# Three tiles per block, two roots together and sums on VectorE alone, in a hybrid decoder layer on one Trainium2 core

## The chip, the cores and the metric

The kernel runs on one core of one Trainium2 chip. The metric is device time in microseconds, the median of several executions. Beside it there is one profiled execution, whose trace gives the rows below. The engines are named as in the profile: PE is TensorE's matmul (PEld its weight load), DVE is VectorE, ACT is ScalarE, POOL is GpSimd, SP is SyncE, whose queue issues the DMAs.

## The reference

One inference step of a one-layer decoder over 1024 prompt tokens and 8 single new tokens, 1032 token columns in all, with a model width of 1024, in f32:

```python
u = rmsnorm(h, norm_mix)
proj = u @ w_in                       # RWKV-7 columns | gated DeltaNet columns | gates
o_a = ...                             # RWKV-7 time mixing from pa
o_b = ...                             # short conv and gated delta rule from pb
mix = gate_a * (o_a @ w_branch_a) + gate_b * (o_b @ w_branch_b)
h = h + mix @ w_out                   # residual
u2 = rmsnorm(h, norm_ffn)
h = h + (silu(u2 @ w_ffn_gate) * (u2 @ w_ffn_up)) @ w_ffn_down
h = h + sigmoid(rmsnorm(h, norm_ple) @ w_ple_gate) * (pe @ w_ple_proj)
y = rmsnorm(h, norm_final)
```

It also returns the new states of both mixers.

## The kernel before

**Layout.** Everything is held transposed: channels on the 128 partitions (KT = 8 channel tiles), tokens along the free dimension. The 1032 columns are cut into three blocks of BW = 344, or for the second half of the kernel into two halves of 516 and four quarters of QW = 258. Each f32 operand of a large product is split into a rounded high part and a rest (`split`, lines 245 to 250, for activations; `halves_of`, line 184, for weights, ScalarE for the high part, GpSimd for the rest), and three products hi·hi, lo·hi, hi·lo are summed. So one weight tile of `w_in` on one block is 24 matmuls of 344 columns. Split weights live in `wsp`, six buffers for each of `wh` and `wl`; a tile of `w_in` takes two of each.

**Order.** A planner orders the instructions of each engine ahead of time, by priority (`tc.cur_priority`, a lower number goes first) and by when it believes each is ready; adding LATER = 100000 puts work behind what is urgent. Each engine then runs its list strictly in order. In the head and in `order` (line 112) TensorE's list is the order in which the code is written.

**The head (lines 355 to 409).** `xs` holds the input. Per block, `gram(g)` puts the Gram matrices of its 128-token pieces on TensorE. `inv` takes the diagonal (product with `idr`, sum), the reciprocal square root by twelve small steps on 128x3 (`rsq`, lines 236 to 242), scales `idr` by it (`nre`, line 290), and a product with `ones` on TensorE spreads the result over all partitions; ScalarE copies it to `R`. `scale(g, R)` multiplies the eight channel tiles of the block by `R`, alternately on VectorE and GpSimd (line 391), and splits them into `xh` and `xl` (lines 249, 250). `stream` yields the products with `w_in` one matmul at a time; `dense_some(n)` lets n of them go. Its first two tiles are done block by block, all later ones tile by tile. The result is evacuated by ScalarE to `gs` and stored. Behind the head, `order` interleaves the rest of this stream with the two mixers.

**The residual and the FFN's input (lines 1436 to 1500).** `mixer_out(t)` does, for each half t, the product with `w_out` and the residual: VectorE adds x to the product (`H<-acc`, line 1468), the squares are summed over the channel tiles (`square`, line 1415), and a root as above gives `RN[t]`. `mixes(t)` scales H by `RN[t]` (line 1443, 8 operations of 516 columns) and forms the seven inputs of a Strassen product: 20 sums `ms` (line 1453) and 28 rests `xl` (line 1456) of 258 columns, alternately on VectorE and GpSimd, and 28 rounded copies on ScalarE. Between, the product with `w_ple_proj` (`dense(a["wpp"])`) runs; ScalarE evacuates it to `po`, two buffers of one block each, and SP stores it (lines 1497 to 1499). Then come the gate and up products (`strassen`): seven products per half, each of 12 matmuls of 258 columns; the first gate product takes the whole first half before the second.

**The FFN.** After a group of hidden tiles the product with `w_ffn_down` is added to the residual: each block is loaded into a tile `a`, added to (line 1611) and stored. `depth[0]` is the number of buffers of `a`.

Of the kernel before, what the change touches and what calls it, by code (L numbers as in the profile page):

```python
# [58 lines left out]
def hybrid(ctx, tc, a, o):  # L59
# [145 lines left out]
    def width(c):  # L205
        return c.stop - c.start
# [55 lines left out]
            G.tensor_copy(idr[:, t0:min(n, t0 + P)], ident[:, :min(P, n - t0)])  # L262
        return idr

    def inv_rms(R, ps, pl_, newps, grams=False):

        n = ps.shape[1]  # L270
        parts = [slice(t0, min(n, t0 + P)) for t0 in range(0, n, P)]
        e = pl_.tile([P, idr.shape[1]], F32, tag="nre", name="nre", bufs=2)
        r = pl_.tile([P, 3, 3], F32, tag="nrr", name="nrr", bufs=2)
        if grams:
            V.memset(r[:, 0], 1.0)
            for i, c in enumerate(parts):
                w = slice(0, width(c))
                tt(e[w, c], ps[w, c], idr[w, c], MULT)
                V.tensor_reduce(r[w, 0, i:i + 1], e[w, c], AX.X, ADD)
        else:  # L280
            tt(e[:, :n], ps, idr[:, :n], MULT)
            if n >= 2 * P:
                V.tensor_reduce(r[:, 0, 0:2], e[:, 0:2 * P].rearrange("p (i t) -> p i t", t=P), AX.X, ADD)
            for i, c in enumerate(parts):
                if n < 2 * P or i > 1:
                    V.tensor_reduce(r[:, 0, i:i + 1], e[:, c], AX.X, ADD)
        q = [r[:, i, :len(parts)] for i in range(3)]
        rsq(q[1], q[0], 1.0 / T, EPS, q[0], q[2])
        for i, c in enumerate(parts):
            ts(e[:, c], idr[:, c], r[:, 1, i:i + 1], None, MULT)  # L290
        pr = newps([P, n])
        mm(pr, ones, e[:, :n], start=True, stop=True)
        act(R, pr, AF.Copy)

    def stream(jobs):
# [38 lines left out]
            if b == NBLK - 1:  # L334
                mark(("pa", ti), 3.0)

        nxt = [fetch(ti) for ti in jobs[:2]]
        for b in range(NBLK):
            for ti, w in zip(jobs, nxt):
                yield from product(ti, *w, b)  # L340
        for n, ti in enumerate(jobs[2:], 2):
            if n == 2:
                nxt = fetch(ti)
            w = nxt
            tc.cur_priority -= LATER
            if n + 1 < len(jobs):
                nxt = fetch(jobs[n + 1])
            tc.cur_priority += LATER
            for b in range(NBLK):
                yield from product(ti, *w, b)  # L350
# [6 lines left out]
    with tc.tile_pool(name="ld", bufs=1, side="right", reuse_waits="tile") as ld, \  # L357
# [20 lines left out]
                    mm(ps[:w, t0:t0 + w], x, x, start=(k == 0), stop=(k == KT - 1))  # L378
            return ps

        def inv(g, ps):
            R = ld.tile([P, BW], F32, tag="R0", name="R0", bufs=2)
            tc.cur_priority -= 2 * LATER
            inv_rms(R, ps, ld, ft, True)
            tc.cur_priority += 2 * LATER
            return R

        def scale(g, R):
            c = cols(g)
            for k in range(KT):  # L390
                (gtt if k % 2 else tt)(xs[:, k, c], xs[:, k, c], R, MULT)
                split(xs[:, k, c], vc("nmix", k), xh[k][:, c], xl[k][:, c])

        def dense_some(n):
            for _ in range(n):
                next(dense_in)

        s0 = gram(0, ct([P, BW]))
        s1 = gram(1, ct([P, BW]))
        scale(0, inv(0, s0))  # L400
        dense_some(3 * KT)
        s2 = gram(2, st1([P, BW]))
        R = inv(1, s1)
        dense_some(3 * KT)
        scale(1, R)
        R = inv(2, s2)
        dense_some(6 * KT)
        scale(2, R)
        dense_some(6 * KT)
    w0h, a0h, kah, ka1 = vx[:, 0:4], vx[:, 4:8], vx[:, 8:12], vx[:, 12:16]  # L410
    ts(w0h, vc("w0", 0, 4), 0.5, None, MULT)
    ts(a0h, vc("a0", 0, 4), 0.5, None, MULT)
# [1023 lines left out]
    def mixes(pl_, t):  # L1436


        hi, lo = ([pl_.tile([P, 4, QW], F32R, tag=f"x{q}{i}", name=f"x{q}{t}{i}") for i in range(7)] for q in "hl")
        tc.cur_priority += LATER  # L1440
        y = []
        for m in range(KT):
            stt(H[t][m], H[t][m], vc("nffn", m), RN[t], MULT, MULT)  # L1443
# [1 line left out]
        for i in SIX:  # L1445
            for k in range(4):
                (y11, y12), (y21, y22) = y[k], y[k + 4]
                p, q, op = ((y11, y22, ADD), (y11, None, None), (y12, y22, SUB), (y21, y11, SUB),
                            (y22, None, None), (y11, y12, ADD), (y21, y22, ADD))[i]
                e, e2 = (gtt, tt) if k % 2 else (tt, gtt)  # L1450
                if op:
                    s = hq[t].tile([P, QW], F32, tag="ms", name="ms", bufs=3)
                    e(s, p, q, op)
                    p = s
                act(hi[i][:, k], p, AF.Copy)
                e2(lo[i][:, k], p, hi[i][:, k].bitcast(F32), SUB)
        tc.cur_priority -= LATER
        return hi, lo

    def mixer_out(t):  # L1460
# [30 lines left out]
    xb = pool(ctx, "xm1", 1)  # L1491
    XM[1] = mixes(xb, 1)
    sgp = pool(hstk, "sg", 1)
    sg = [sgp.tile([P, TOK], F32, name=f"sg{i}") for i in range(2)]
    for m in range(KT):
        def evac(b, ps, m=m):
            y = hq[1].tile([P, BW], F32, tag="po", name="po", bufs=2)
            act(y, ps, AF.Copy)
            SP.dma_start(pp_d[m, :, cols(b)], y)
        dense(a["wpp"][m], 2, ph, pl, evac)  # L1500

# [69 lines left out]
    for n in (2, 4, 4, 4, 4, 4):  # L1573
        for j in range(0, n, 2):
# [11 lines left out]
            if f0 + j == 0:  # L1586
# [1 line left out]
                hp = pool(hstk, "hid")  # L1588
                hh, hl = pair(hp, "hid", 4)
                tmp = pool(hstk, "tf", 2)  # L1590
                depth[0] = 5
            strassen(a["wu"], f0 + j, up)
        final = f0 + n == NF
        if final:
# [133 lines left out]
```

## Time and profile before

| | us |
|---|---|
| median of 3 runs | 2087.26 (2086.81 to 2088.21) |
| profiled execution, its own time | 2085.75 |
| span of its trace | 2084.0 |
| TensorE busy in the span | 1943.8 (93%) |
| VectorE, ScalarE, GpSimd busy | 1321.5, 845.0, 1045.1 |

The time of the profiled execution is 1.75 us more than the span of its trace: what lies around the first and the last instruction. "Busy" counts an operation from its start to its end, including time in which it stands still for a resource; matmuls overlap each other and their ends are modelled. The granted clock (PEclk) is a mean over a window, as a share of full speed; the clock has two levels, 1.2 and 2.4 GHz.

### The profile page before, as it was taken

To read this page: it belongs to the slowest core of one execution; us is meant where nothing else is said; L and a number is where in the kernel's file an instruction comes from. 1 tells how busy PE (TensorE), PEld (TensorE's weight loads), DVE (VectorE), ACT (ScalarE), POOL (GpSimd) and SP (SyncE) were. 2 spreads that over 40 slices of the span, in tenths; PEclk is the share of its full clock that TensorE was granted. 3 is DMA by queue.
4 is the path that set the end of the run, shared out by engine and by line. 5 is a ranking of instruction groups with operands and counts; after the bars stand their busy time and mean duration, and the time that the engine had idled before them with its cause. 6 is when DMAs were issued, how large, how long until landed. Compare 5 with 4: busy or idle time off the path is not lost.

```text
span 2084.0 us, 40641 instructions
## 1 busy us (share of the span) xinstructions
PE 1943.8 (93%) x14904; PEld 1819.6 (87%) x14904; DVE 1321.5 (63%) x3253; ACT 845.0 (41%) x2069; POOL 1045.1 (50%) x1144
## 2 busy tenths in 40 slices
PE   5988999899899997999799988999999999999996
PEld 5987878777777877989699978899999999999995
DVE  6269756987988549736644587464643636446767
ACT  2343353555555341237523355241433414234532
POOL 3366362556564244750047677463645536354722
PEclk8999899999999999999899998999999999999998
DMA  4433332243343433564445542625244262433312
GB/s 143 126 107 107 101 105 89 79 131 93 100 118 112 144 93 119 168 177 126 155 139 168 166 151 75 196 75 165 86 123 143 72 186 69 130 110 113 110 55 95
DMA packets 218497, 250.89 MB, mean 120 GB/s; under 512 B 48409, under 2 KB 176297, under 8 KB 218297
## 3 DMA queue, kind: packets, MB, share of 16 engines
q1 hardware_dynamic: 218296, 248.30, 39.4%
q8 instruction: 117, 1.92, 0.4%
q14 instruction: 84, 0.68, 0.1%
HBM read 170.82 MB, written 77.40 MB: 119 GB/s over the span
## 4 chain that ended last, share of the span: by engine, by line
PE 64%; DVE 21%; DMA 4%; ACT 4%; issue 4%; POOL 3%; SPq 0%; DVEq 0%; POOLq 0%; ACTq 0%
PE acc L75 54%; PE c L75 3%; PE f L75 3%; DVE GM L685 1%; PE zp L75 1%; DVE inv L721 1%; PE f L79 1%; PE s L75 1%; DVE L L574 1%; PE x L75 1%; DVE H L1443 1%; DMA a<-h_d 1%; DVE inv L722 1%; DVE LB L709 1%; DMA out_gdns<-St 1%
## 5 line engine op out<-in xcount | busy, mean ns | idle before, releaser
L75 PE MATMUL acc<-xh,wh 128*128 128x258 f32 (+2 forms) x2360 | 733.3, 311 | 13.1 <-ACT gs L328 5.7
L75 PE MATMUL acc<-xl,wh 128*128 128x258 f32 (+2 forms) x2360 | 728.0, 309 | 9.7 <-DVE xl L250 5.6
L75 PE MATMUL acc<-xh,wl 128*128 128x258 f32 (+1 forms) x2336 | 722.9, 310 | 0.0
L187 POOL TENSOR_TENSOR wl<-ws,wh 128x512 fp32r<-128x512 f32 (+1 forms) x256 | 334.7, 1309 | 440.2 <-ACT wh L186 408.3
L75 PEld LDWEIGHTS acc<-xh,wh 128*128 128x128 f32 (+1 forms) x2360 | 450.7, 191 | 22.8 <-ACT gs L328 6.0
L75 PEld LDWEIGHTS acc<-xl,wh 128*128 128x128 f32 (+1 forms) x2360 | 451.2, 191 | 18.3 <-DVE xl L250 6.4
L75 PEld LDWEIGHTS acc<-xh,wl 128*128 128x128 f32 x2336 | 448.5, 192 | 5.8 <-POOL wl L187 0.5
L186 ACT ACTIVATE wh<-ws 128x512 fp32r<-128x512 f32 (+1 forms) x256 | 157.2, 615 | 257.7 <-PE acc L75 217.3
L187 POOL TENSOR_TENSOR wl<-s,wh 128x512 fp32r<-128x512 f32 x110 | 145.0, 1320 | 124.4 <-ACT wh L186 123.6
L75 PE MATMUL acc<-hidh,wh 128*128 128x344 f32 x528 | 167.1, 320 | 4.6 <-DVE a L1611 4.0
L75 PE MATMUL acc<-hidl,wh 128*128 128x344 f32 x528 | 169.5, 321 | 0.0
L75 PE MATMUL acc<-hidh,wl 128*128 128x344 f32 x528 | 168.8, 320 | 0.0
L1611 DVE TENSOR_TENSOR a<-a,acc 128x344 f32<-128x344 f32 x120 | 60.9, 512 | 137.7 <-PE acc L75 92.8
L186 ACT ACTIVATE wh<-s 128x512 fp32r<-128x512 f32 x110 | 69.2, 630 | 141.0 <-PE acc L75 98.0
L1561 POOL TENSOR_TENSOR s<-ws 128x512 f32<-128x512 f32 x66 | 87.7, 1329 | 48.1 <-DMA ws<-in_wg 34.9
L75 PEld LDWEIGHTS acc<-hidh,wh 128*128 128x128 f32 x528 | 98.8, 188 | 6.8 <-DVE a L1611 5.2
L75 PEld LDWEIGHTS acc<-hidl,wh 128*128 128x128 f32 x528 | 99.3, 188 | 0.3 <-DVE hidl L247 0.3
L75 PEld LDWEIGHTS acc<-hidh,wl 128*128 128x128 f32 x528 | 99.3, 188 | 0.0
L445 POOL TENSOR_TENSOR cy<-cy,cu 128x344 f32<-128x344 f32 x72 | 68.8, 955 | 50.2 <-ACT cu L444 44.1
L75 PE MATMUL acc<-mxh,wh 128*128 128x258 f32 x256 | 72.7, 284 | 0.0
L75 PE MATMUL acc<-mxl,wh 128*128 128x258 f32 x256 | 72.6, 284 | 0.0
L75 PE MATMUL acc<-mxh,wl 128*128 128x258 f32 x256 | 72.2, 282 | 0.0
(464 smaller groups left out, 4074.2 us busy)
## 6 DMA issues: line engine op xcount, KB each, us to landing
ws<-in_win SPq DMA_DIRECT2D x92, 256.0 KB, 3.1
a<-h_d SPq DMA_DIRECT2D x120, 172.0 KB, 2.6
h_d<-a SPq DMA_DIRECT2D x120, 172.0 KB, 2.8
pa_d<-gs SPq DMA_DIRECT2D x90, 172.0 KB, 2.2
ws<-in_wg SPq DMA_DIRECT2D x44, 256.0 KB, 2.9
ws<-in_wu SPq DMA_DIRECT2D x44, 256.0 KB, 3.0
ws<-in_wd SPq DMA_DIRECT2D x40, 256.0 KB, 2.7
gate_d<-gs SPq DMA_DIRECT2D x48, 172.0 KB, 2.7
```

The lines of the kernel that those rows point to most:

```text
L75: last[0] = TE.matmul(out, w, x, start=start, stop=stop).ins
L79: last[0] = TE.transpose(out, x, ident).ins
L186: act(h, s, AF.Copy)
L187: (eng or gtt)(l, s, h.bitcast(F32), SUB)
L445: gtt(y, y, u, ADD)
L574: V.tensor_tensor_scan(L[:, c * C:c * C + C], ones[:, 0:C], L[:, c * C:c * C + C], 0.0, MULT, ADD)
L685: stt(GM[:, 2 * (c + j) + h], ps[h][:, j], cvf[:, cg, h:h + 1], rwmask, MULT, MULT)
L709: V.transpose(LB[0:32, i0:i0 + 16], G2[:, :, i0:i0 + 16].rearrange("p b i -> p i b"))
L721: tt(u[:, :i], XB[:, :i, :i], LB[:, 16 + i:17 + i, 16:16 + i].to_broadcast([P, i, i]), MULT)
L722: tt(w, XA[:, :ns, :nj], LB[:, i:i + 1, :nj].to_broadcast([P, ns, nj]), MULT)
L1561: e(s, A_[p], A_[q], op)
L1611: tt(y, y, ps, ADD)
```

## The change

- In the head, `inv` is replaced by `roots`, which takes a list of Gram blocks: the root of block 0 is taken alone, those of blocks 1 and 2 in one chain whose small steps work on 128x6. The three Gram products come first, and roots and first norming stand in a higher priority band. `scale` uses VectorE for all eight tiles.
- `stream` does three tiles block by block instead of two; `dense_some` is called with 6, 12 and 9 times KT matmuls between the steps, 216 in all instead of 144.
- `mixes` does all sums and rests on VectorE, and the first half's stand one more LATER behind (`(2 - t) * LATER`).
- `po` becomes two full-width tiles that later hold `sg`.
- The FFN's `a` has six buffers instead of five.

```diff
-        nxt = [fetch(ti) for ti in jobs[:2]]
+        nxt = [fetch(ti) for ti in jobs[:3]]
         for b in range(NBLK):
             for ti, w in zip(jobs, nxt):
                 yield from product(ti, *w, b)
-        for n, ti in enumerate(jobs[2:], 2):
-            if n == 2:
+        for n, ti in enumerate(jobs[3:], 3):
+            if n == 3:
                 nxt = fetch(ti)
...
-        def inv(g, ps):
-            R = ld.tile([P, BW], F32, tag="R0", name="R0", bufs=2)
-            tc.cur_priority -= 2 * LATER
-            inv_rms(R, ps, ld, ft, True)
-            tc.cur_priority += 2 * LATER
+        def roots(grams):
+
+            n = len(grams)
+            parts = [(g, i, min(P, BW - i * P), slice(i * P, min(BW, i * P + P))) for g in range(n) for i in range(3)]
+            e = ld.tile([P, n, BW], F32, name=f"e{n}")
+            r = ld.tile([P, 3, 3 * n], F32, name=f"r{n}")
+            V.memset(r[:, 0], 1.0)
+            for g, i, w, c in parts:
+                tt(e[:w, g, c], grams[g][:w, c], idr[:w, c], MULT)
+                V.tensor_reduce(r[:w, 0, 3 * g + i:3 * g + i + 1], e[:w, g, c], AX.X, ADD)
+            rsq(r[:, 1], r[:, 0], 1.0 / T, EPS, r[:, 0], r[:, 2])
+            R = []
+            for g, i, w, c in parts:
+                ts(e[:, g, c], idr[:, c], r[:, 1, 3 * g + i:3 * g + i + 1], None, MULT)
+                if i == 2:
+                    pr = ft([P, BW])
+                    mm(pr, ones, e[:, g], start=True, stop=True)
+                    R.append(ld.tile([P, BW], F32, name=f"R{n}{g}"))
+                    act(R[-1], pr, AF.Copy)
             return R

         def scale(g, R):
             c = cols(g)
             for k in range(KT):
-                (gtt if k % 2 else tt)(xs[:, k, c], xs[:, k, c], R, MULT)
+                tt(xs[:, k, c], xs[:, k, c], R, MULT)
                 split(xs[:, k, c], vc("nmix", k), xh[k][:, c], xl[k][:, c])
...
+        tc.cur_priority -= 2 * LATER
         s0 = gram(0, ct([P, BW]))
         s1 = gram(1, ct([P, BW]))
-        scale(0, inv(0, s0))
-        dense_some(3 * KT)
+        R0, = roots([s0])
         s2 = gram(2, st1([P, BW]))
-        R = inv(1, s1)
-        dense_some(3 * KT)
-        scale(1, R)
-        R = inv(2, s2)
+        scale(0, R0)
+        tc.cur_priority += 2 * LATER
         dense_some(6 * KT)
-        scale(2, R)
-        dense_some(6 * KT)
+        tc.cur_priority -= 2 * LATER
+        R1, R2 = roots([s1, s2])
+        scale(1, R1)
+        tc.cur_priority += 2 * LATER
+        dense_some(12 * KT)
+        scale(2, R2)
+        dense_some(9 * KT)
...
-        tc.cur_priority += LATER
+        tc.cur_priority += (2 - t) * LATER
         y = []
...
-                e, e2 = (gtt, tt) if k % 2 else (tt, gtt)
                 if op:
                     s = hq[t].tile([P, QW], F32, tag="ms", name="ms", bufs=3)
-                    e(s, p, q, op)
+                    tt(s, p, q, op)
                     p = s
                 act(hi[i][:, k], p, AF.Copy)
-                e2(lo[i][:, k], p, hi[i][:, k].bitcast(F32), SUB)
-        tc.cur_priority -= LATER
+                tt(lo[i][:, k], p, hi[i][:, k].bitcast(F32), SUB)
+        tc.cur_priority -= (2 - t) * LATER
...
-    sg = [sgp.tile([P, TOK], F32, name=f"sg{i}") for i in range(2)]
     for m in range(KT):
-        def evac(b, ps, m=m):
-            y = hq[1].tile([P, BW], F32, tag="po", name="po", bufs=2)
-            act(y, ps, AF.Copy)
-            SP.dma_start(pp_d[m, :, cols(b)], y)
+        po = sgp.tile([P, TOK], F32, tag=f"sg{m % 2}", name="po")
+
+        def evac(b, ps, m=m, po=po):
+            act(po[:, cols(b)], ps, AF.Copy)
+            SP.dma_start(pp_d[m, :, cols(b)], po[:, cols(b)])
         dense(a["wpp"][m], 2, ph, pl, evac)
+    sg = [sgp.tile([P, TOK], F32, tag=f"sg{i}", name=f"sg{i}") for i in range(2)]
...
-                depth[0] = 5
+                depth[0] = 6
```

## Rows read from the trace of the kernel before

**Rows 1.** Windows of the head: each engine's busy time, clock, DMA share, GB/s.
```profile
17.40:30.20 12.80, 2.87 (x7) 1.15 (x5) 12.65 (x24) 6.75 (x13) 11.14 (x10) 0.62 0.27 83
30.20:44.40 14.20, 14.17 (x94) 13.83 (x94) 7.82 (x21) 2.77 (x6) 4.16 (x4) 0.87 0.16 49
44.40:58.00 13.60, 5.92 (x19) 5.31 (x19) 11.21 (x28) 5.62 (x12) 5.38 (x6) 0.62 0.04 14
58.00:82.00 24.00, 24.00 (x155) 24.00 (x154) 9.33 (x25) 8.20 (x17) 9.93 (x11) 1.00 0.45 141
```

**Rows 2.** TensorE's waits from 0 to 125 us: total, times, longest.
```profile
PE f L75 <- DVE nre L290: 7.7, 1, 7.7
PE acc L75 <- DVE xl L250: 5.6, 2, 3.1
```

**Rows 3.** Head: first root's window on VectorE, then single timeline rows (start, length).
```profile
12.60:17.00 4.40, 3.82 (x21) 1.00 1.06 371
...
18.07 0.46 ACT L293 ACTIVATE R<-f 128x344 f32<-128x344 f32 x1 [0.70 <-PE f L75]
24.84 0.50 DVE L391 TENSOR_TENSOR xs<-xs,R 128x344 f32<-128x344 f32 x1
28.46 1.22 DVE L240 TENSOR_TENSOR nrr<-nrr 128x3 f32<-128x3 f32 x1
58.22 4.66 DVE L250 SCALAR_TENSOR_TENSOR xl<-xs,vec,xh 128x344 fp32r<-128x344 f32 x8
...
26.56 4.75 POOL L187 TENSOR_TENSOR wl<-ws,wh 128x512 fp32r<-128x512 f32 x3 [1.66 <-ACT wh L186]
...
35.19 4.98 PE L75 MATMUL s<-xs 128*128 128x128 f32 x48
```

**Rows 4.** ScalarE's timeline: two evacuations of the first stage, three products apart.
```profile
74.61 0.46 ACT L328 ACTIVATE gs<-acc 128x344 f32<-128x344 f32 x1 [3.01 <-issue]
...
85.95 0.46 ACT L328 ACTIVATE gs<-acc 128x344 f32<-128x344 f32 x1 [3.01 <-issue]
```

**Rows 5.** Windows from the second half's residual to the first down products.
```profile
1185.00:1213.70 28.70, 28.70 (x237) 28.47 (x236) 23.77 (x30) 13.38 (x34) 27.88 (x28) 1.00 0.49 145
1213.70:1231.20 17.50, 10.51 (x64) 9.85 (x63) 14.97 (x32) 9.57 (x25) 16.00 (x22) 1.00 0.48 155
1231.20:1258.00 26.80, 24.53 (x153) 23.17 (x153) 23.86 (x40) 16.19 (x39) 18.62 (x15) 0.94 0.44 145
1258.00:1290.00 32.00, 25.90 (x167) 24.27 (x168) 22.01 (x36) 15.93 (x42) 28.34 (x31) 0.79 0.19 57
1303.00:1331.00 28.00, 24.05 (x141) 22.12 (x142) 10.53 (x22) 2.19 (x5) 3.47 (x4) 1.00 0.72 216
```

**Rows 6.** TensorE's waits from 1200 to 1290 us.
```profile
PE acc L75 <- POOL xl L1456: 3.6, 2, 2.1
PE acc L75 <- ACT po L1498: 3.4, 3, 1.6
PE f L75 <- DVE c L1428: 2.9, 1, 2.9
PE f L75 <- DVE nre L290: 2.6, 1, 2.6
```

**Rows 7.** Busy in 1185:1290, VectorE (then GpSimd), of lines 1443, 1453 and 1456.
```profile
1185.00:1290.00 105.00, 17.39 (x16) 0.92 0.38 120
...
1185.00:1290.00 105.00, 17.12 (x20) 15.94 (x20) 0.92 0.38 120
...
1185.00:1290.00 105.00, 23.63 (x28) 25.02 (x28) 0.92 0.38 120
```

**Rows 8.** Shortest, median and longest ns of a scaling and of a sum.
```profile
L1443 DVE SCALAR_TENSOR_TENSOR H<-H,vec,R x16: 746/1180/1782, 1185.1 to 1248.4; 128x516 f32<-128x516 f32 x16
...
L1453 DVE TENSOR_TENSOR ms<-H x8: 415/665/1184, 1216.5 to 1280.8; 128x258 f32<-128x258 f32 x8
```

**Rows 9.** TensorE's wait for the down product's tile, 1300 to 1345 us.
```profile
PE acc L75 <- DVE a L1611: 4.0, 6, 1.3
```

More of the change, by code (lines that the diff above doesn't have):

```diff
@@ L263, in diagonal, with inv_rms @@
         return idr
-    def inv_rms(R, ps, pl_, newps, grams=False):
+    def inv_rms(R, ps, pl_, newps):
         n = ps.shape[1]
@@ L273, in inv_rms @@
         r = pl_.tile([P, 3, 3], F32, tag="nrr", name="nrr", bufs=2)
[L274 to L286, printed above, removed]
+        tt(e[:, :n], ps, idr[:, :n], MULT)
+        if n >= 2 * P:
+            V.tensor_reduce(r[:, 0, 0:2], e[:, 0:2 * P].rearrange("p (i t) -> p i t", t=P), AX.X, ADD)
+        for i, c in enumerate(parts):
+            if n < 2 * P or i > 1:
+                V.tensor_reduce(r[:, 0, i:i + 1], e[:, c], AX.X, ADD)
         q = [r[:, i, :len(parts)] for i in range(3)]
```

## The prediction

> **What bounds the kernel now.** I read the page first: TensorE is busy 93% of the span and the chain that ended last runs mostly through its products, so time is won only where TensorE stands still or runs at its lower clock. Two places touched by the change have such holes.
>
> The first is the head. In the windows [rows 1] TensorE works 2.87, 14.17 and 5.92 us in the 40.6 us from 17.4 to 58: 17.6 us idle. The granted clock there is 0.62, 0.87 and 0.62, so part of the work ran at the lower of two levels (1.2 instead of 2.4 GHz); with about 11 us of work at half speed that is another 5.6 us. From 58 on it is busy without a gap at clock 1.00. The waits [rows 2] name the causes: 7.7 us for `nre` (the second and third root) and 5.6 us for `xl` (the split of the normed input). Both come from VectorE.
>
> The second is the stretch from the second half of the residual to the first gate product. Its windows [rows 5] show TensorE idle 7.0 us (1213.7 to 1231.2), 2.3 us (1231.2 to 1258) and 6.1 us (1258 to 1290), 15.4 us in all, at clocks 1.00, 0.94 and 0.79. Work at the lower level costs about 5.5 us more (a mean of 0.79 over 32 us is 13 us at half clock, of which I count 8 with work; 0.94 over 26.8 is another 3.2). The waits [rows 6] are mixed: `po` 3.4, the sum of squares 2.9, `nre` 2.6, `xl` of the sums 3.6.
>
> **The head, step by step.** Until R of block 0 is written at 18.5 [rows 3] the order is the same. After that three things move.
>
> (a) The norming of a block loses GpSimd. On VectorE one channel tile costs 0.50 for the product and 0.58 for `xl` (8 in 4.66) [rows 3], so 8 tiles take 8.6 us. Before, small steps of the second root were sown in between, and several waited for a GpSimd operation: a 128x3 product took 1.22 us [rows 3]. Now the roots come behind, but the weight splits on GpSimd remain: three took 4.75 us with two VectorE operations let in at each [rows 3]. Block 0 would end at 27.1 with no such block and at 32 with all four splits in the way; I take 31, since most of them find VectorE at work.
>
> (b) The second and third root are one chain. The first root's 21 operations (three products, three sums, twelve small steps, three diagonals) take nearly all of a 4.4 us window [rows 3], some 0.205 us each with their gaps. Of two roots, 12 + 12 + 3 = 27 come before the first diagonals are whole: 5.5 us, so 36.5, and with the spreading product and the copy R at 38.4. TensorE meanwhile does the third Gram block (4.98 us [rows 3]) under the norming instead of behind it at 35.2, and the 24 products of the second tile while the roots run. Their 3.8 us may be 6 at the lower clock; that still ends near 37.
>
> (c) Three tiles per block instead of two. While VectorE norms block 1 (38.4 to 47.0), TensorE has the third tile of block 0 to do; then the first tile of block 1 follows the norming to about 47.5, and two more tiles cost 7.6 us. A tile of 24 products costs 3.78 us (three between the starts of two evacuations, 74.61 and 85.95 [rows 4]). Block 2 is normed from 47 to 55.6 under these, so nothing waits, and its three tiles end at 55.1 + 11.3 = 66.4. The ninth product of a tile and block was done before at 85.95 - 3.78 = 82.2 [rows 4]. The same work is done **16 us** sooner.
>
> Bounds: with no GpSimd block it is 20. If GpSimd blocks all along and 72 products run at the slow stretch's 0.31 us each (5.92 us for 19 [rows 1]) instead of 0.1575, it is 16 - 2 - 11 = 3. Three tiles take all six weight buffers, so the fourth tile is split only when the first is through (58); two splits at 1.6 us fit ahead of 66, so this costs nothing, and 3 us if not. The third tile's loads and splits were issued early before too; SP's queue gets no new work. R, `e` and `r` have own buffers: no wait is added.
>
> **The sums and the residual.** Removed: 20 sums and 28 `xl` on GpSimd, 15.9 + 25.0 us [rows 7]. Added on VectorE: the same 48. Alone, such an operation takes VectorE 0.42 us, but beside GpSimd the mean was (17.12 + 23.63)/48 = 0.85 [rows 7, 8]; a scaling of H takes 0.75 alone, 1.09 in the mean. So the whole is 16 x 0.75 + 96 x 0.42 = 52 us of VectorE in place of the 58 it spends now on its half. This is the core of the change: VectorE does twice the operations in less time if GpSimd lets go.
>
> Here a page speaks against it. The Trainium skill, Perfetto Trace Analysis, section Optimizing Scalar/DVE Operations, says that offloading to Scalar or even GpSimd can make sense where VectorE is saturated, and adds that the shared read port may spoil it. By its first half the change goes the wrong way, and the sum would end at rival 3's 2090 instead of 2058. The 0.85 beside GpSimd against 0.42 alone [rows 7, 8] agrees with its second half.
>
> Priority: the first half's sums now stand behind everything of the residual, `po` and gate stage; what waits on VectorE are `H<-acc` and the root of the second half. The latter's chain has the same small steps as the head's, which pay up to 1.22 us beside GpSimd [rows 3]; freed, I let it end some 8 us sooner. By wait: `po` goes (3.4: two full-width tiles hold six blocks where two did, so a store has a whole weight tile's 18 products, 2.8 us at the head's pace, in which to land); the sum of squares goes (2.9); `nre` and the sums' waits (2.6 and 6.6 together [rows 6] with the smaller ones) halve. That is 10 to 11; of the 5.5 us of low clock I give back 2. One wait is added: the gate's first write to `sg` waits for the last stores of `po`, with ScalarE's copies queued behind it; it comes two Strassen products (24 x 0.121 = 2.9 us, from 237 in 28.7 [rows 5]) after the last of them, about as long as a store may take, so I price it at 0 to 1 and within the rest. I take **12 us**. Bounds: 0 (the wait only moves) and 21 (all idle and slow time gone).
>
> **FFN buffers.** Depth six instead of five for `a`: TensorE waited 4.0 us for `a` [rows 9] in a stretch where 24 blocks took 28.0 us, 24.05 of them busy [rows 5]. It moved 216 GB/s with 0.72 of the DMA time, so a sixth load ahead helps only partly: **1.5 us**, bounds 0 and 4. In the later groups TensorE is busy throughout, and nothing is to be had.
>
> **Sum.** 16 + 12 + 1.5 = 29.5. Against the profiled execution's own 2085.75 us (span 2084.0 and 1.75 around it) this is 2056.3; the median of the runs is 1.5 above the profiled one, so 2057.8, say **2058**. All bounds together give 2042 to 2084.
>
> **Rivals.**
> 1. *The head pays, the sums don't* (2070): the wait moves from the sums of the second half to those of the first, since these are now last in line. For: TensorE needs them first. Against: VectorE is idle 5 of the 28.7 us before 1213.7 [rows 5], and its sums can start long before the second half's root.
> 2. *The head pays little* (2066 to 2069, gain 5 to 8 there): TensorE, fed one channel tile per us, stays at the lower clock. For: before, it came back only near 58 after the last hole [rows 1]. Against: it is fed more densely now.
> 3. *VectorE becomes the bound* (2090, no change to be told): its 84.6 us of busy time in 105 [rows 5] grow by 48 x 0.85 = 41, to 20 more than the stretch has. It needs 0.85 to stay, though GpSimd loses 41 of its 91 us. The Trainium skill's rule on offloading (Perfetto Trace Analysis, Optimizing Scalar/DVE Operations) points this way.
> 4. *Slower* (2094): the planner puts all of the first half's 26 us of VectorE work behind the second half's. The second's R would come near 1235, its 26 us end at 1261, the first's at 1287. Gate and up need 28 x 12 products of 0.121 us (237 in 28.7 us [rows 5]) = 41 us, so 1327 instead of 1303: 24 lost against 17.5 won. It decides from 17.5 us on, that is if over two thirds of the first half are left at 1235.
> 5. *Nothing comes out* (within 0.2%): the head's gain is given back at TensorE's next wait, the features of the first head pair. Against: those hang on a product of the same stream (its loads follow the product's store), which moves along.
>
> **How the numbers follow.** Chances: forecast 0.64 (own range 2046 to 2068), rival 1 0.17, rival 2 0.08, rival 3 0.04, rival 4 0.04, rival 5 0.03. To leave out no more than 2 in 10, the range takes in rivals 1 and 2 and the upper half of the gains: 2044 to 2076. 0.2% (4 us) is about what this measurement can tell. Faster: 0.64 + 0.17 + 0.08 = 0.89; same: 0.04 + 0.03 = 0.07; slower 0.04.
>
> **What would show it.** Right: the ninth product ends near 66 instead of 82; TensorE idles under 8 us between 17 and 58; `po` vanishes from its waits; VectorE's mean for a sum is near 0.5; the stretch that ended at 1303 ends near 1275. Wrong: low clock or a wait for `xl` past 45; a wait for `xl` of the first half ahead of the gate products; sums at 0.8 us on VectorE; or the head's 16 us lost again by 200.

## The result and the profile after

The changed kernel takes 2073.25 us in the median of 15 runs (2064.53 to 2083.17) against 2086.81 for 15 runs of the kernel before: ratio 0.9937, 95% interval 0.9918 to 0.9956. It is faster by 13.6 us; 29 were forecast. Its profiled execution took 2082.16 us (span 2080.3), so it is one of its slowest, and the first thing to find out is why.

A table of leads orders what follows. Five instructions that every kernel executes serve as marks; a lead is the start in the trace of the kernel before minus the start in the other trace, in us. Each kernel has one trace, so a stage of it is one sample; the unaltered change, traced twice, differs from itself by 0.5 at most, but kernels with the same head and the same list behind it differ by 2.5 at A and by 8 at B. The gain or loss of a stage is the difference of two neighbours.

| kernel (of runs below) | A: 14th copy to `gs` (before: 101.05) | B: 113th copy to `gs` (812.01) | C: first `c<-a,acc` (1072.17) | D: first down add (1304.05) | E: 61st down add (1563.47) |
|---|---|---|---|---|---|
| the change | 12.8 | 26.2 | 11.7 | 12.3 | 4.7 |
| the change again (e5) | 12.6 | 25.8 | 11.2 | 12.0 | 4.8 |
| e1 five buffers | 13.2 | 27.9 | 26.8 | 26.3 | 25.8 |
| e2 head only | 12.8 | 26.1 | 22.0 | 21.8 | 21.7 |
| e3 old priority | 13.1 | 24.5 | 21.5 | 22.9 | 16.1 |
| e4 sums on both | 14.9 | 25.7 | 22.0 | 18.1 | 12.1 |
| e6 sixth buffer only | 0.5 | 1.5 | 4.0 | 3.3 | -5.6 |
| e7 weights first | 13.6 | 32.2 | 31.0 | 30.4 | 31.3 |
| e8 head and `po` | 13.4 | 31.8 | 20.4 | 16.8 | 16.5 |
| e9 head, two tiles | 7.2 | -3.1 | -2.7 | -0.9 | -2.1 |
| e10 head, split norming | 7.2 | 17.3 | 12.8 | 12.8 | 12.9 |
| e11 weight sums on GpSimd | 12.6 | 28.5 | 26.7 | 28.0 | 29.0 |
| e12 rests on GpSimd | 12.9 | 27.6 | 26.4 | 23.1 | 23.1 |
| e13 third tile only | 3.7 | 21.0 | 16.8 | 16.3 | 15.9 |
| e14 weights first, five buffers | 15.1 | 32.6 | 27.1 | 26.6 | 24.8 |
| e15 head, weights first | 13.5 | 31.9 | 27.7 | 27.5 | 29.3 |

So the change won 12.8 at the head and 13.4 more by B, lost 14.5 between B and C, won 0.6 in the residual and gate stage (C to D), lost 7.6 in the first down stage (D to E).

**The head.** Windows of the changed kernel, for [rows 1]:

```profile
17.40:30.20 12.80, 9.42 (x62) 8.30 (x62) 12.80 (x21) 6.55 (x14) 8.48 (x6) 0.82 0.39 116
30.20:44.40 14.20, 11.47 (x64) 10.79 (x62) 11.45 (x40) 7.97 (x18) 0.00 (x0) 0.92 0.13 45
44.40:58.00 13.60, 13.25 (x73) 12.83 (x74) 8.57 (x25) 2.93 (x7) 0.00 (x0) 0.87 0.13 40
```

TensorE idles 6.5 us before 58 where it idled 17.6, and the wait for `nre` of [rows 2] is gone. VectorE's timeline shows what keeps the second block:

```profile
37.70 6.50 DVE L397 TENSOR_TENSOR xs<-xs,R 128x344 f32<-128x344 f32 x15 [2.30 <-ACT R L391]
44.12 1.55 DVE L250 SCALAR_TENSOR_TENSOR xl<-xs,vec,xh 128x344 fp32r<-128x344 f32 x3
45.58 0.51 DVE L397 TENSOR_TENSOR xs<-xs,R 128x344 f32<-128x344 f32 x1
46.01 6.42 DVE L250 SCALAR_TENSOR_TENSOR xl<-xs,vec,xh 128x344 fp32r<-128x344 f32 x13
```

Fifteen of both blocks' sixteen products run in one go, since both `R` are there together, and the rests that block 1 needs come only behind them. Block 1's first tile is evacuated at 50.44.

**Residual to gate.** TensorE's waits from 1200 to 1290, for [rows 6]:

```profile
PE acc L75 <- DVE xl L1464: 7.0, 5, 2.4
PE f L75 <- DVE c L1437: 6.8, 1, 6.8
PE acc L75 <- ACT x L1533: 1.2, 1, 1.2
```

Windows of all engines, for [rows 5]:

```profile
1171.00:1200.00 29.00, 29.00 (x242) 28.95 (x242) 28.05 (x45) 13.39 (x33) 19.37 (x18) 1.00 0.43 128
1200.00:1218.00 18.00, 11.18 (x61) 10.71 (x60) 14.28 (x43) 10.62 (x29) 8.42 (x9) 0.81 0.50 151
```

VectorE's busy time in lines 1452 (scaling), 1461 (sums) and 1464 (rests), for [rows 7]:

```profile
1160.00:1290.00 130.00, 19.05 (x16) 0.93 0.40 121
...
1160.00:1290.00 130.00, 22.67 (x40) 0.93 0.40 121
...
1160.00:1290.00 130.00, 29.25 (x56) 0.93 0.40 121
```

`po` is gone from the waits. In its place TensorE waits 6.8 us in one piece for the sum of squares: VectorE is full (28.05 of 29 us) with the first half's sums, and the last residual adds stand among them. TensorE's timeline has the last matmul of the residual's product (`mxh`) and the end of the wait:

```profile
1200.21 0.28 PE L75 MATMUL acc<-mxh,wl 128*128 128x258 f32 x1
...
1209.68 1.23 PE L75 MATMUL f<-c,cs 128*128 128x258 f32 x2 [6.82 <-DVE c L1437]
```

The add that this sum of squares needs runs only at 1207.86, with sums and rests around it. Then the second half's root meets something else. VectorE's timeline:

```profile
1207.86 0.41 DVE L1476 TENSOR_TENSOR H<-acc,a 128x258 f32<-128x258 f32 x1
1208.19 0.41 DVE L1461 TENSOR_TENSOR ms<-H 128x258 f32<-128x258 f32 x1
1208.53 0.42 DVE L1464 TENSOR_TENSOR xl<-ms,xh 128x258 fp32r<-128x258 f32 x1
1208.87 0.41 DVE L1461 TENSOR_TENSOR ms<-H 128x258 f32<-128x258 f32 x1
1209.21 0.42 DVE L1437 TENSOR_TENSOR c<-c,sq 128x258 f32<-128x258 f32 x1
...
1214.81 0.16 DVE L241 SCALAR_TENSOR_TENSOR nrr<-nrr 128x3 f32<-128x3 f32 x1
1217.74 0.69 DVE L1570 TENSOR_TENSOR s<-ws 128x512 f32<-128x512 f32 x1 [2.77 <-DMA ws<-in_wg]
1218.35 1.26 DVE L242 SCALAR_TENSOR_TENSOR nrr<-nrr 128x3 f32<-128x3 f32 x1
...
1230.38 9.59 DVE L1452 SCALAR_TENSOR_TENSOR H<-H,vec,R 128x516 f32<-128x516 f32 x8 [1.87 <-ACT R L285]
```

A sum of gate weights that have not landed stands in the middle of the root's small steps for 2.77 us.

**The first down stage.** TensorE's waits from 1290 to 1345, for [rows 9]:

```profile
PE acc L75 <- ACT wh L186: 8.8, 1, 8.8
PE acc L75 <- DVE a L1620: 1.9, 3, 1.3
```

SP's timeline of issues there, and the row of GpSimd's that waits for the last of them:

```profile
1288.20 0.33 SPq L1520 DMA_DIRECT2D ws<-in_wg  x1
1292.33 1.57 SPq L1626 DMA_DIRECT2D h_d<-a  x2
...
1319.89 0.32 SPq L1626 DMA_DIRECT2D h_d<-a  x1
1320.26 0.43 SPq L1520 DMA_DIRECT2D ws<-in_wg  x1
...
1323.47 1.26 POOL L1570 TENSOR_TENSOR s<-ws 128x512 f32<-128x512 f32 x1 [25.82 <-DMA ws<-in_wg]
```

The wait for `a` halves, from 4.0 to 1.9. But the last weights of the next gate pair are issued at 1320.26, behind 21 of the 24 stores of `a`, and TensorE stands 8.8 us for them.

**The 14.5 us between B and C.** Windows of the changed kernel:

```profile
850.00:860.00 10.00, 8.72 (x109) 6.71 (x109) 5.27 (x11) 1.36 (x3) 6.49 (x9) 0.58 0.44 123
860.00:870.00 10.00, 10.00 (x102) 7.68 (x103) 2.99 (x8) 1.64 (x3) 8.79 (x12) 0.50 0.64 197
870.00:880.00 10.00, 10.00 (x86) 7.83 (x87) 2.29 (x8) 2.22 (x4) 6.88 (x11) 0.50 0.49 156
880.00:890.00 10.00, 10.00 (x90) 7.83 (x90) 0.42 (x1) 2.89 (x5) 3.89 (x5) 0.50 0.24 69
890.00:900.00 10.00, 10.00 (x85) 8.79 (x82) 0.74 (x3) 2.23 (x4) 6.42 (x8) 0.70 0.42 98
```

The same windows of e2, the head alone, whose TensorE works off the same list here at nearly the same times:

```profile
850.00:860.00 10.00, 8.30 (x107) 6.50 (x108) 5.69 (x11) 1.61 (x4) 6.49 (x9) 0.59 0.37 120
860.00:870.00 10.00, 10.00 (x125) 7.87 (x124) 2.98 (x8) 2.66 (x5) 8.45 (x12) 0.73 0.68 186
870.00:880.00 10.00, 10.00 (x144) 7.79 (x143) 2.29 (x8) 3.64 (x7) 8.11 (x12) 1.00 0.51 147
```

Both drop to the lower level where TensorE has short waits (8.72 and 8.30 of 10 us busy). In e2 the clock is back by 870; in the change it stays at 0.50 into the last window, with TensorE busy all the time. From B to C the change loses 14.5 us and e2 4.1. Of the others with three tiles e8 comes nearest: its clock is at 0.50 from 850 to 880, and it loses 11.4; the rest lose 1.1 to 5.5.

### The profile page after: what moved, and what is told of

Same layout as the page of the kernel before. It is cut to its first block, busy times and chain, and to the rows that moved or that the text cites. A ratio compares the mean times of both kernels' runs of the same rounds, so it can differ in the third digit from the quotient of the medians.

```text
span 2080.3 us, 40640 instructions
## 1 busy us (share of the span) xinstructions
PE 1953.9 (94%) x14904; PEld 1826.7 (88%) x14904; DVE 1326.4 (64%) x3300; ACT 847.1 (41%) x2069; POOL 995.5 (48%) x1084
## 4 chain that ended last, share of the span: by engine, by line
PE 55%; DVE 14%; issue 4%; ACT 3%; DMA 2%; POOL 1%; SPq 0%; DVEq 0%; ACTq 0%; POOLq 0%
PE acc L75 48%; PE f L75 2%; PE c L75 1%; DVE xl L1464 1%; PE f L79 1%; PE x L75 1%; DVE ms L1461 1%; DVE inv L731 1%; DVE H L1452 1%; PE zp L75 1%; ACT uxh L249 1%; DVE tm L1085 1%; DVE GM L694 1%; DVE U L1620 0%; PE o L75 0%
## 5 line engine op out<-in xcount | busy, mean ns | idle before, releaser
L75 PE MATMUL acc<-xl,wh 128*128 128x258 f32 (+2 forms) x2360 | 737.2, 313 | 13.5 <-DVE xl L1464 7.0
L75 PEld LDWEIGHTS acc<-xl,wh 128*128 128x128 f32 (+1 forms) x2360 | 456.2, 193 | 23.4 <-DVE xl L1464 8.2
L454 POOL TENSOR_TENSOR cy<-cy,cu 128x344 f32<-128x344 f32 x72 | 70.4, 978 | 48.8 <-ACT cu L453 47.4
```

Source lines behind the costliest of these rows:

```text
L75: last[0] = TE.matmul(out, w, x, start=start, stop=stop).ins
L454: gtt(y, y, u, ADD)
```

## The experiments

**First four: which part of the change gives what.** All start from the changed kernel; e1, e3 and e4 alter one thing in it, e2 keeps its head alone. e1:

```diff
-                depth[0] = 6
+                depth[0] = 5
```

> The changed kernel with five buffers for the down product's tile instead of six. Theory A (the sixth buffer harms): six loads ahead put the next group's gate weights behind nearly all loads and stores in SP's queue; with five the 8.8 us wait for wh ahead of the second group disappears, and from the first to the 31st block of the down products about 7 us less pass; median near 2066. Theory B (the sixth buffer helps by about 1.5 us as predicted, and the 8.8 us wait has another cause, the earlier start of the group): the wait stays, TensorE waits some 2 us more for the tile, median 2074 to 2076.

e2 has the change's head and the kernel before's sums, priority, `po` and five buffers.

> Only the head of the change: two roots together, norming on VectorE, three tiles per block. Sums, priority, po and five buffers as before. Theory A (the head is all of the gain, sums and po together give nothing, the sixth buffer takes away 7): the ninth product ends near 69.6 as in the changed kernel, 12.8 us earlier than before; the stretch from the second half's residual to the first down product takes as long as before within 2 us; median 2066 to 2070, below the changed kernel's 2073. Theory B (sums and po give most of their 12 us, and the profile of the changed kernel misleads): median 2074 or above, and the stretch is some 10 us longer than in the changed kernel.

e3:

```diff
-        tc.cur_priority += (2 - t) * LATER
+        tc.cur_priority += LATER
...
-        tc.cur_priority -= (2 - t) * LATER
+        tc.cur_priority -= LATER
```

> The changed kernel with the first half's sums at the old priority. Theory A (VectorE's fixed list puts the sums before the last residual additions in either case, because it falls behind the plan): the 6.8 us wait for the sum of squares at the end of the residual stays between 4 and 9 us and the median lies within 3 us of the changed kernel. Theory B (the lower priority shields the residual): without it the wait grows to 12 us or more, and the median is 5 us or more higher.

e4 keeps the low priority and divides the sums between the engines again:

```diff
+                e, e2 = (gtt, tt) if k % 2 else (tt, gtt)
...
-                    tt(s, p, q, op)
+                    e(s, p, q, op)
...
-                tt(lo[i][:, k], p, hi[i][:, k].bitcast(F32), SUB)
+                e2(lo[i][:, k], p, hi[i][:, k].bitcast(F32), SUB)
```

> The changed kernel with the sums and rests alternating between VectorE and GpSimd again, low priority kept. Theory A (taking GpSimd away gains nothing in sum): the stretch from the second half's residual to the first down product is within 3 us of the changed kernel's, median within 3 us. Theory B (VectorE alone is faster, as predicted): the second half's last rest is written 8 us or more later, the stretch is 8 us or more longer, and the median rises by as much.

| | median, us | ratio to before, interval |
|---|---|---|
| e1 five buffers | 2063.02 | 0.9875, 0.9849 to 0.9900 |
| e2 head only | 2061.31 | 0.9870, 0.9840 to 0.9901 |
| e3 old priority | 2069.15 | 0.9907, 0.9882 to 0.9932 |
| e4 sums on both engines | 2075.32 | 0.9928, 0.9901 to 0.9955 |

The head alone gives at least all that the change gives (the change measured a second time, e5 below, has 0.9893). With five buffers D to E costs 0.5 (e1) and 0.1 (e2), with six 6.8 (e3) and 6.0 (e4). C to D gives -0.5 (e1), -0.2 (e2, nothing of the new sums) and +1.4 (e3): with the wide `po` the sums' 12 us don't come, at either priority. The low priority changes nothing that the traces show: TensorE's wait for the sum of squares is 6.7 us with the old one (e3) and 6.8 with the new. The median of e3 is still 4 us below the change's, where its expectation allowed 3. With the sums divided the stage loses 3.9 (e4), where it won 0.6 in the change; e8 below tells why.

**Next four: the sixth buffer, `po`, and the low clock.** e5 is the changed kernel unaltered.

> The changed kernel once more, unaltered, as the control for the three beside it, and to see whether the 40 us at a granted clock of 0.50 around 855 us of its first trace belong to the kernel or to that execution. If they come and go (my theory: the four other kernels with the same instruction order there showed 7 to 14 us of low clock), its trace now shows under 20 us of them and the profiled time is 2062 to 2072; if they belong to the kernel, 2080 to 2084 again. Median 2073 by both, since it is a median over executions of both kinds.

2067.08 (2060.84 to 2081.07), ratio 0.9893, 0.9866 to 0.9920. Its profiled execution, 2081.07, shows the long low clock again, so my forecast of its trace failed. Its other five runs took 2060.84 to 2073.10. Each run's mean granted clock is on record: 0.970 to 0.971 in the four up to 2067.96, 0.963 in that of 2073.10, 0.959 in the profiled one. So time at the low clock does differ from execution to execution of this kernel; where the others had theirs no trace shows.

e6 is the kernel before with `depth[0] = 6`.

> The kernel before with nothing but the sixth buffer for a. The prediction's term (a sixth load ahead saves 1.5 us of the 4.0 that TensorE waits for a) gives 1.5 us less than the kernel before. The theory from the first experiments (the deeper queue of loads stands ahead of the gate weights of the next group in SP's fixed order, and TensorE then waits for these) gives 6 to 10 us more than the kernel before, with a wait of 7 us or more for wh in the first down stage.

2092.40, ratio 1.0019, 1.0002 to 1.0035: slower by a little. D to E loses 8.9 and TensorE waits 8.6 for `wh`, with nothing else of the change in it. The prediction's +1.5 has the wrong sign.

e7 keeps six buffers and moves only the loads of the second group's first gate pair:

```diff
+        first = src is a["wg"] and j == 2
-        tc.cur_priority += LATER
+        tc.cur_priority += 0 if first else LATER
         for i, q in ((0, 0), (1, 1), (1, 0), (0, 1)):
             A_[i, q] = (wst if i == q else sp).tile([P, 4, P], F32, tag="ws", name="ws")
             SP.dma_start(A_[i, q], src[j + i][:, 4 * q:4 * q + 4])
-        tc.cur_priority -= LATER
+        tc.cur_priority -= 0 if first else LATER
```

> The changed kernel, six buffers kept, with the four weight loads of the second group's first gate pair one priority band higher, so that SP issues the last of them after 3 of the stores of the down stage and not after nearly all of them. If SP's order is what the sixth buffer costs: the wait of 8.8 us for wh is gone, the block 31 of the down stage comes 5 to 8 us sooner after the first one, and the median lies 5 to 10 us under that of the unaltered change beside it (2063 to 2068 where that has 2073). If the sixth buffer costs by something else (DMA bandwidth shared by more loads, VectorE's order), the wait moves to another tile and the median stays within 3 us of the change's.

2055.33 (2053.60 to 2063.14), ratio 0.9847, 0.9821 to 0.9873, the best version so far, 12 us below the unaltered change beside it. Its waits in the down stage:

```profile
PE acc L75 <- DVE a L1621: 3.1, 5, 1.1
PE acc L75 <- ACT wh L186: 0.6, 1, 0.6
```

D to E turns from -7.6 to +0.9. SP's order is what the sixth buffer cost. Of the 12 us some 8 are this (-7.2 in e5, +0.9 here). Where the rest of the medians' difference lies is not shown; the two profiled executions differ by 20 us before C, most of it low clock from 860 to 900 (granted 1.00 here, 0.55 in e5).

e8 is e2 with the two wide `po` tiles.

> The head of the change and the two wide tiles for po; the sums, their priority and five buffers as before. If the 3.2 us that TensorE waited for po in the run with the head alone are worth their time, the stage from the residual's c to the first down product is 2 to 3 us shorter than there (which was as before) and the median 2058 to 2060. If another wait takes their place, as it did with the sums on VectorE, the stage stays within 1 us and the median at 2061.

2067.51, ratio 0.9903, 0.9876 to 0.9929. C to D loses 3.6. TensorE's waits from 1190 to 1290 in e2:

```profile
PE acc L75 <- POOL xl L1465: 3.4, 2, 2.1
PE acc L75 <- ACT po L1507: 3.2, 3, 1.6
PE f L75 <- DVE nre L282: 2.6, 1, 2.6
PE f L75 <- DVE c L1437: 2.5, 1, 2.5
```

And in e8:

```profile
PE f L75 <- DVE nre L282: 5.2, 1, 5.2
PE acc L75 <- ACT x L1534: 2.7, 1, 2.7
PE acc L75 <- DVE xl L1465: 1.5, 2, 0.8
```

TensorE is through with the `po` products sooner and stands for the root instead: short waits for `po` and the sum of squares become one long one for `nre`. The waits together are hardly longer, but the clock is a little lower. From C to D TensorE does the same 1644 matmuls in both; e2, then e8:

```profile
1050.20:1282.20 232.00, 214.33 (x1644) 209.52 (x1643) 153.21 (x294) 103.93 (x245) 167.00 (x173) 0.96 0.46 139
...
1051.80:1287.30 235.50, 216.58 (x1644) 212.53 (x1643) 155.10 (x295) 104.84 (x245) 166.09 (x173) 0.95 0.46 137
```

Of the 3.5 us more, 1.2 are idle time, and in 2.3 the same matmuls run longer. Both branches of the expectation missed. e4 has these waits too (`nre` 5.2 in one piece), so its loss is that of the wide `po` beside divided sums, at either priority. VectorE's sums with the narrow `po` were not run.

**Next four: the head's parts, VectorE's list.** e9 is e2 with two tiles per block, e10 is e2 with the norming's product on both engines:

```diff
-        nxt = [fetch(ti) for ti in jobs[:3]]
+        nxt = [fetch(ti) for ti in jobs[:2]]
...
-        dense_some(12 * KT)
+        dense_some(6 * KT)
...
-        dense_some(9 * KT)
+        dense_some(6 * KT)
```

> The head alone as in the earlier run, but with two tiles of products per block instead of three. The prediction's step (c) says that the third tile is what fills TensorE while VectorE norms the next block. If so: TensorE idles 3.8 us more in each of two normings, the products done at 82 us are 5 to 8 us later than with three tiles, and this much of the head's gain is gone (gain at 82 us 5 to 8 instead of 12.8). If the roots' order and VectorE alone make the gain, it stays at 11 to 13.

```diff
-                tt(xs[:, k, c], xs[:, k, c], R, MULT)
+                (gtt if k % 2 else tt)(xs[:, k, c], xs[:, k, c], R, MULT)
```

> The head alone, three tiles per block, with the norming's product alternating between GpSimd and VectorE as before. The prediction's step (a) lets VectorE alone be the faster: then the blocks are normed 1 us or so later each and the gain at 82 us falls by 2 to 4. The rival, that GpSimd's weight splits and ScalarE's copies set the pace of the first block anyway (its 8 channel tiles came every 1.5 us, and not every 1.08) and that three tiles hide the rest, gives the same gain within 1 us.

e9: 2083.86, ratio 0.9990, 0.9970 to 1.0010: no gain that can be told. e10: 2067.19, 0.9904, 0.9877 to 0.9930. Both lead by 7.2 at A (for e10 that is 5.6 less than in e2, where 2 to 4 were expected), yet at B one is 3.1 behind and the other 17.3 ahead. e9 keeps a wait of the kernel before that e2, e10 and the change don't have. TensorE's longest wait from 760 to 830 in the kernel before:

```profile
PE f L79 <- DVE tm L1076: 9.0, 1, 9.0
```

It is 9.0 us in e9 too; in e2 the longest there is 1.1. A window there of the kernel before:

```profile
780.00:820.00 40.00, 29.31 (x188) 28.07 (x188) 35.87 (x85) 6.35 (x14) 12.35 (x12) 0.87 0.34 104
```

Of e9:

```profile
780.00:820.00 40.00, 29.31 (x186) 27.34 (x185) 33.98 (x82) 7.04 (x15) 12.10 (x12) 0.87 0.33 100
```

Of e2:

```profile
780.00:820.00 40.00, 39.30 (x247) 38.72 (x248) 37.45 (x74) 8.97 (x18) 21.81 (x24) 1.00 0.53 165
```

The reason is in the code. The planner `order` starts where the head leaves the stream of products, after 144 of them with two tiles and after 216 with three. With two, TensorE's list behind the head is that of the kernel before, but for a few exchanged neighbours; with three, the mixers' steps stand elsewhere among the products. The old list waits 9 us for `tm`, in the kernel before and in e9; the new one has products to do in that place. The head's lead of e9 is gone before that (3.5 at 323 us, 0.2 at 566), and not by waits. From A to B TensorE does the same 5296 matmuls in the kernel before, e9 and e2:

```profile
101.00:812.00 711.00, 651.78 (x5296) 555.27 (x5295) 538.34 (x1554) 320.99 (x803) 357.33 (x511) 0.96 0.35 105
...
93.90:815.10 721.20, 662.38 (x5296) 563.63 (x5295) 536.28 (x1555) 322.49 (x804) 355.36 (x511) 0.94 0.34 104
...
88.30:786.00 697.70, 650.26 (x5296) 552.29 (x5295) 529.00 (x1526) 321.84 (x804) 355.62 (x511) 0.97 0.35 107
```

Its idle time is 59.2, 58.8 and 47.4 us. So the new list saves 11.8 us of idle time there, and e9 loses its lead by the lower clock alone (0.94 for 0.96), in an execution that was the slowest of its ten.

e11 and e12 start from e7. e11 takes the weight sums `s` of the first gate pair (there `apart` is true) off VectorE; e12 the first half's rests:

```diff
-                e(s, A_[p], A_[q], op)
+                (gtt if apart else e)(s, A_[p], A_[q], op)
```

> The change with the gate weights' loads one band higher, as in the run of that name, and all four sums of weights of the first gate pair on GpSimd, none on VectorE. In that run's trace VectorE stands 3.2 us in the middle of the second half's root, behind such a sum whose weights have not landed. If that chain sets the end of the stage (root, scaling, sums of the second half, then TensorE's waits for xl of 6.4 us): the waits for xl shrink by 2 to 4 us, and the median by as much, to 2051 to 2054. If TensorE's first wait there (5.0 us for the sum of squares, VectorE being full before) sets it, nothing changes within 1.5 us.

```diff
-                tt(lo[i][:, k], p, hi[i][:, k].bitcast(F32), SUB)
+                (tt if t else gtt)(lo[i][:, k], p, hi[i][:, k].bitcast(F32), SUB)
```

> The same base, with the 28 rests xl of the first half's sums on GpSimd and only its 20 sums on VectorE; the second half stays on VectorE. If VectorE is full when the residual of the second half comes (it worked 28 of 29 us there in the change): the last residual adds and the sum of squares come earlier, the wait of 5.0 to 6.8 us for the sum of squares falls under 3 us, and the stage to the first down product is 2 to 4 us shorter. If the two engines slow each other down as in the kernel before (0.85 us for an operation that takes 0.42 alone), the wait stays or moves to the first half's rests, and the median is the same or up to 3 us higher.

e11: 2055.19, ratio 0.9839, 0.9815 to 0.9864, the same as e7. C to D goes from -0.6 to +1.3, and the waits for `xl` from 6.4 to 5.3: the stall in the root's steps costs 1 to 2 us, not 2 to 4. TensorE's wait for the sum of squares is 7.0 there (5.0 in e7) and stays the first one.

e12: 2059.88, 0.9869, 0.9844 to 0.9894. The wait for the sum of squares is gone, as the theory of the full VectorE says, but 4.7 us for `nre` stand in its place and C to D loses 3.3, where e7 lost 0.6. So VectorE was full, and emptying it on GpSimd's account pays nothing.

**Last three: what stayed open.** e13 is the kernel before with the third tile and nothing else:

```diff
-        nxt = [fetch(ti) for ti in jobs[:2]]
+        nxt = [fetch(ti) for ti in jobs[:3]]
...
         R = inv(1, s1)
-        dense_some(3 * KT)
+        dense_some(6 * KT)
         scale(1, R)
         R = inv(2, s2)
-        dense_some(6 * KT)
+        dense_some(9 * KT)
         scale(2, R)
-        dense_some(6 * KT)
+        dense_some(9 * KT)
```

> The kernel before with nothing but three tiles of products per block at the head (roots one by one and norming on both engines as before). If the order of TensorE's list behind the head makes the larger part (that list is then the one of the changed kernel): the wait of 9.0 us for tm near 785 is gone, and though the head itself gains little (2 to 6 us at 100 us), the kernel is 10 to 18 us faster than before. If the roots and VectorE's norming carry the gain, it is within 5 us of the kernel before and the wait for tm stays.

2073.69, ratio 0.9928, 0.9900 to 0.9956: 10.8 us faster with 3.7 at A. The wait of 9.0 us for `tm` is gone (from 760 to 830 the longest is 1.1), and 14 of the 21.0 us at B come after 225 us (lead 6.9 there), 8.5 of them between 777 and 812. With the norming and roots of e2 on top, B has 26.1: the new list is the larger part.

e14 is e7 with five buffers, e15 is e2 with six buffers and e7's loads.

> The change with the second group's gate weights one band higher, as before, but with five buffers for a. The prediction priced the sixth buffer at 1.5 us of gain; with the weights out of its way it can show it: then five buffers give 1 to 3 us more time than the 2055 measured with six. If the sixth buffer is worth nothing, it is within 1.5 us; if earlier weights alone were the gain, with five buffers it is even faster.

> The head of the change, six buffers and the gate weights one band higher, with the sums, their priority and po as before the change. If sums and po on the new paths give nothing (the theory from the stage's marks: +0.5, -0.5 and -0.2 us in the change, with five buffers, and with the head alone), the median is that of the same kernel with the new sums, 2055, within 3 us. If they give the prediction's 12 us and something hid it, it is 2060 or more.

e14: 2061.13, ratio 0.9876, 0.9848 to 0.9904. e15: 2061.09, 0.9878, 0.9847 to 0.9909. D to E is +0.9, +1.0 and +1.7 with six buffers and early weights (e7, e11, e15), -1.7 with five (e14) and -0.5 and -0.1 with five and the old loads (e1, e2). So in these traces the sixth buffer is worth 1 to 3 us once it delays nothing. The medians lie 6 us from e7's: e15's was expected within 3 if the new sums and `po` give nothing, and missed that. But the intervals overlap and C to D is the same (-0.5, -0.1, -0.6): that the new sums, priority and `po` together give something here is not shown.

## Why the prediction was wrong

**The head (16 us): right in kind, 12.8 in size.** The ninth product ends near 69.5 (the eighth is evacuated at 65.91, and a tile takes 3.77) and not at 66.4. Step (a) fits: block 0 is normed at 31.2, 31 had been taken. Step (b) fits: R of block 1 is there at 37.7, against 38.4. Step (c) is the mis-sized one: it had block 1 normed by itself to 47.0 and its first tile following to 47.5; in VectorE's list most of block 2's products come ahead of block 1's rests, and the tile was evacuated at 50.44, which is the 3 us that are missing. The third tile, the roots and the VectorE norming each matter at A: 3.7 with the third tile alone, 7.2 without it, 7.2 with the norming divided, 12.8 with all.

**What the head sets free behind it: left out.** The prediction let a lead be kept or lost as a whole (rival 5). In the change it was neither. With the old list it is lost by 570 us (e9, to the clock); the third tile's new list doubles it by 812 (26.1 in e2, 17.3 in e10, 21.0 in e13). The prediction took the third tile as filler for the head only, not as a new starting point for the planner.

**The sums (12 us): the step that failed.** "Twice the operations in less time if GpSimd lets go" was half right: 40 sums take 0.57 and 56 rests 0.52 us in the mean, against 0.85; but the 16 scalings take 1.19, not 0.75, and the total is 71.0 us, not 52, against 58.1 before. It fits, but not where it matters: the first half's sums fall in the 29 us before the second half's last residual adds and fill VectorE there. That the residual's add and the root are what waits on VectorE was right. But the prediction took the lower priority to keep the first half's sums out of their way, and the adds now wait in the list behind those sums, with the lower priority as without it (6.8 and 6.7 us, e3). The 3.4 of `po`, 2.9 of the sum of squares, 2.6 of `nre` and 3.6 of `xl` became 6.8 and 7.0. C to D gave 0.6: rival 1's time (2070), by a wait for the first half's work, as it said, though for the adds behind the sums and not for the sums themselves. The number near rival 1's is luck: a head that gave less, a gain behind it that nobody foresaw and the loss in the FFN happen to cancel. One part of the change pays for another here: beside divided sums the wide `po` loses 3.6 (e8) or 3.9 (e4, low priority), and VectorE alone brings that back to nothing. Rival 3's price, 0.85 kept, did not come true. The Trainium skill (Perfetto Trace Analysis, section Optimizing Scalar/DVE Operations) says that offloading may make sense where VectorE is saturated, but may not help between VectorE and GpSimd because of the shared read port; the traces agree with the second half: after e12's offload from a VectorE that was full the stage lost 3.3 us, against 0.6 without it. What the port has to do with that no run shows.

**The FFN (+1.5 us): wrong in sign, -7.6.** The term saw the wait for `a`, and that wait did shrink by 2.1. It did not ask what stands behind the deeper queue of loads on SP: the next group's weights. e6 shows it alone, e7 takes it away.

**The sum.** From the change's own stages, with e2's loss of 4.1 between B and C in place of the profiled 14.5: 12.8 + 13.4 - 4.1 + 0.6 - 7.6 = 15.1; behind E another 1.0 is lost. That is near the 13.6 of the medians, but an estimate: which loss between B and C the median run had no trace shows. Forecast was 16 + 0 + 0 + 12 + 1.5. Two terms were off by 20 together, and an unseen gain of 9 covered half of that. The best version run, with the weights first, takes 2055. Of the prediction's signs of being right three came true (6.5 us idle, `po` gone, a sum at 0.57 us), but D stands at 1291.8 and not near 1275: the signs were of parts, and a part gained nothing where another wait took its place.

## What to carry to other kernels

A deeper buffer moves every transfer queued behind its loads, and a longer head moves where a planner starts: for each such edit, look at what comes next in that engine's list, not at the wait alone. Freeing one engine's operations of a neighbour's interference gained nothing in sum here, since the work landed where that engine was full, so read the window just ahead of the critical operation before pricing the sum. And when a change moves the time less than forecast, marks on the same instruction in both traces show which stage gave it back.

## What the runs showed of the chip

In the change TensorE ran at its lower level (0.50) from about 850 to 896 while the profile shows it busy all the time from 860 on: 86 matmuls from 870 to 880 at 0.50, where e2 did 144 at 1.00. With the same list, e2 was back at the higher level before 870. The Trainium skill (TensorE: Matmul & The Clock Gate, section What's actually happening) says that throttling is the default and activity releases it; the traces agree only in part, since in the change the level stayed low through 36 us of gapless work, where e2's rose after some 5 us of it. Why is not shown by these runs. Both profiled executions of the change had it, and e8 some 34 us of it; the other fourteen traces had at most 21 us there.
